# A list scheduler that holds a PSUM bank as one piece, and each block's attention put right ahead of its own FFN, in a one-core decoder step

## The chip, the core and the metric

One core of a Trainium2 chip runs the whole program. Its engines work side by side, each through its own queue in order: TensorE (PE, matmuls; its weight loads are shown as PEld), VectorE (DVE), ScalarE (ACT), GpSimd (POOL) and SyncE (SP), which issues every DMA. The metric is the device time of one execution in microseconds (us), lower is better.

## What is computed

One step of a hybrid decoder layer for a prompt of 2048 tokens and 8 decode tokens, all in float32, D = 1024. Cut to what matters:

```python
def decoder_layer(x, ...):
    y, ... = parallel_mixer(rms_norm(x, norm_mix), ...)      # conv module (31 taps) beside gated DeltaNet, 4 heads
    x = x + y                                                # y = concat(conv, delta) @ w_out
    x = x + memory_attend(rms_norm(x, norm_mem_q), mem_k, mem_v, w_mq, w_mo)   # 4 heads, 256 memory tokens
    x = x + swiglu(rms_norm(x, norm_ffn), w_gate, w_up, w_down)                # D_FF = 2816
    return x, ...
# and rms_norm(x, norm_f) at the end; the decode tokens attend to 8 cached memories of 256 tokens
```

## The kernel before, in words

The prompt is cut into 4 blocks of 512 tokens (`NB`, `TB`). First the mixer runs over two pairs of blocks (PE tiles `hd`, `glua`, `glub` for the projections; `pk`, `pq`, `pu`, `pch`, `po` for the DeltaNet chunks). Then each block has three more steps: the output projection ("out", PE tile `rg` reading `catS`), the memory attention ("att": scores `sc`, softmax, transposes `ppt`, and the product with the values, PE tile `rg` reading `pT`), and the FFN (`fx`, `fy`, `fz` for gate and up, `dn` for down). The FFN is a Strassen-like scheme: its right operands `op` are halves and differences (`xn`, `tt`) that DVE and ACT build from the normalised block. Every large weight is split into two float32r parts, a high one by ACT and a low one by POOL or DVE (tile `w` from `raw`). The decode attention (`kt`, `scs`, `psc`, `podd`) runs as one more lane beside the FFN of block 0.

The Python code writes no instruction at once. `Tape` records all of them with their operands (`add`, L165) in program order, and `Tape.order` (L283) then lays them out by list scheduling: it walks a clock of its own for each engine with the costs of `cost` (L176) and the latencies `LAT`, takes for each engine the ready operation with the smallest key, and the order in which operations are taken is the order in which each engine's queue receives them. What is ready follows from `graph` (L227): reads and writes of a tile depend on each other where their boxes (`box`, L207) overlap. In a PSUM tile, which is one bank, two column ranges are so two independent pieces, and nothing in the planner stops one engine from reading a bank while another writes another part of it. The program itself does not run that way: in the trace no two engines are ever in one PSUM tile at the same time.

Program order around the change: `att_plan` and `out_plan` (L855 to L872) put the weights in the order out(0), att(0), out(1), att(1), FFN(0), out(2), att(2), FFN(1), out(3), att(3), FFN(2), held `dn` of FFN(2), FFN(3); the loop at the end of `hybrid_step` (L2754 to L2780) runs the same order. `ffn_norm` (L2536) builds the operands `op` of a block's FFN as a lane of its own; its wait `may` holds it back until the FFN ahead is done and the next block's scores are taken. `dec_attend` (L2286) waits for free tiles of the `t2` pool. `chj` (L1668, L1680, L1810) is the unused output of ACT's squares, in a single buffer.

## Time and profile before

| | us |
|---|---|
| median of 3 runs (3053.68 to 3060.42) | 3055.63 |
| the profiled execution | 3056.0 |
| its span, first to last instruction | 3054.3 |
| PE busy in it | 2958.2 (97%) |
| DVE / POOL / ACT busy | 1971.5 / 1380.7 / 1325.6 |

The mean granted TensorE clock is 0.988 of full speed. A table of windows gives, for each stretch of the span, the busy time of each engine in it with the number of its instructions, the granted clock (PEclk, 1.00 is 2.4 GHz, 0.50 is 1.2 GHz), the DMA engines' share and what they moved. A waits view says which engine sat idle ahead of which tile, and what it had waited for. A timeline lists instructions in order of time; in brackets stands the idle time just before and its releaser. All instructions carry one line, L450, since the tape issues them all there; so they are told apart by tiles.

### The profile page before, as it was taken

What the parts mean: (1) busy time and instruction counts of PE and PEld (TensorE: products, weight loads), DVE (VectorE), ACT (ScalarE), POOL (GpSimd) and SP (SyncE); (2) the same over time, 40 slices, a digit from 0 to 9 for tenths busy, and PEclk for the clock granted to TensorE, in tenths of its full rate; (3) what the DMA queues carried; (4) which work ended last, traced back from release to release, by engine and by line L of the source; (5) the groups of instructions that cost most, each with busy time, mean ns of one, the idle gap of its engine ahead of it and who ended that gap; (6) DMA issues with size and microseconds to landing.
All of it is one profiled execution on the core that took longest, in us unless ns stands there. A gap on an engine that the chain in (4) does not pass through costs nothing.

```text
span 3054.3 us, 52803 instructions
## 1 busy us (share of the span) xinstructions
PE 2958.2 (97%) x18950; PEld 2625.0 (86%) x18950; DVE 1971.5 (65%) x3946; ACT 1325.6 (43%) x2695; POOL 1380.7 (45%) x1228
## 2 busy tenths in 40 slices
PE   8999989999999999989999999999999999999998
PEld 6898867888888878789988779988878999999997
DVE  7857888888986876687678885423576333553334
ACT  6643337543565343545455354333444332433333
POOL 3433333432446455678877204355512443444444
PEclk9999989999999999999999999999999999999999
DMA  6443334543676442277667748766534766676663
GB/s 232 153 131 101 116 114 142 160 147 96 189 255 188 134 140 80 89 245 265 233 251 262 238 136 283 253 227 232 180 117 145 241 215 218 207 244 221 220 221 109
DMA packets 358631, 567.24 MB, mean 186 GB/s; under 512 B 56832, under 2 KB 155072, under 8 KB 358352
## 3 DMA queue, kind: packets, MB, share of 16 engines
q1 hardware_dynamic: 358368, 563.86, 55.9%
q8 instruction: 150, 2.46, 0.3%
q14 instruction: 113, 0.93, 0.1%
HBM read 455.68 MB, written 108.64 MB: 185 GB/s over the span
## 4 chain that ended last, share of the span: by engine, by line
PE 72%; DVE 7%; DMA 4%; ACT 1%; issue 1%; POOL 1%; SPq 0%; POOLq 0%; DVEq 0%; ACTq 0%
PE dn L450 16%; PE fy L450 12%; PE rg L450 9%; PE fz L450 8%; PE fx L450 8%; PE sc L450 5%; PE hd L450 4%; DVE cacc L450 2%; PE pu L450 2%; PE glub L450 1%; PE glua L450 1%; DVE bit L450 1%; PE pch L450 1%; DMA Tm<-zt 1%; DMA w<-sums 1%
## 5 line engine op out<-in xcount | busy, mean ns | idle before, releaser
L450 POOL TENSOR_TENSOR w<-raw,w 128x512 fp32r<-128x512 f32 x683 | 931.4, 1369 | 955.0 <-ACT w L450 866.7
L450 ACT ACTIVATE w<-raw 128x512 fp32r<-128x512 f32 x912 | 568.3, 631 | 942.9 <-PE dn L450 231.9
L450 PE MATMUL dn<-ff,w 128*128 128x512 f32 (+2 forms) x2688 | 518.2, 346 | 0.8 <-ACT ffs L450 0.8
L450 PEld LDWEIGHTS dn<-ff,w 128*128 128x128 f32 x2688 | 421.5, 188 | 58.8 <-ACT ffs L450 1.0
L450 PE MATMUL fy<-op,w 128*128 128x256 f32 (+1 forms) x3168 | 426.8, 283 | 0.5 <-DMA w<-sums 0.5
L450 PEld LDWEIGHTS fy<-op,w 128*128 128x128 f32 x3168 | 403.0, 189 | 8.5 <-issue 1.4
L450 PE MATMUL hd<-hT,w 128*128 128x512 f32 (+2 forms) x1920 | 399.6, 359 | 8.8 <-ACT w L450 6.6
L450 DVE SCALAR_TENSOR_TENSOR cacc<-cu,cw,cacc 128x512 f32<-128x512 f32 x480 | 358.7, 747 | 16.2 <-ACT cacc L450 11.0
L450 PEld LDWEIGHTS hd<-hT,w 128*128 128x128 f32 x1920 | 306.4, 191 | 52.6 <-ACT w L450 6.8
L450 PE MATMUL fz<-op,w 128*128 128x256 f32 (+1 forms) x2112 | 286.4, 282 | 4.2 <-DMA w<-sums 2.1
L450 PE MATMUL fx<-op,w 128*128 128x256 f32 (+1 forms) x2112 | 285.7, 283 | 2.9 <-DVE op L450 1.6
L450 PEld LDWEIGHTS fx<-op,w 128*128 128x128 f32 x2112 | 270.9, 189 | 12.8 <-DVE op L450 2.1
L450 PEld LDWEIGHTS fz<-op,w 128*128 128x128 f32 x2112 | 265.9, 189 | 8.9 <-issue 3.9
L450 DVE TENSOR_TENSOR w<-raw,w 128x512 fp32r<-128x512 f32 x229 | 217.8, 959 | 69.6 <-ACT w L450 67.3
L450 DVE TENSOR_TENSOR x<-dn,x 128x512 f32<-128x512 f32 (+1 forms) x248 | 139.8, 567 | 174.9 <-PE dn L450 172.5
L450 POOL TENSOR_TENSOR sqj<-sqj,sqj 128x512 f32<-128x512 f32 (+1 forms) x98 | 130.2, 1328 | 266.9 <-ACT sqj L450 264.7
L450 PE MATMUL sc<-w,hT 128*128 128x512 f32 x768 | 193.2, 404 | 3.0 <-DVE w L450 1.8
L450 PE MATMUL rg<-catS,w 128*128 128x512 f32 (+2 forms) x960 | 191.9, 355 | 1.9 <-DVE x L450 1.9
L450 PE MATMUL rg<-pT,w 128*128 128x512 f32 x768 | 190.6, 399 | 0.3
L450 PEld LDWEIGHTS rg<-catS,w 128*128 128x128 f32 x960 | 153.9, 189 | 26.9 <-DVE x L450 2.2
L450 PEld LDWEIGHTS sc<-w,hT 128*128 128x128 f32 x768 | 142.7, 191 | 37.6 <-ACT pr L450 3.1
L450 PEld LDWEIGHTS rg<-pT,w 128*128 128x128 f32 x768 | 141.4, 188 | 33.6 <-ACT pr L450 3.0
(381 smaller groups left out, 4036.3 us busy)
## 6 DMA issues: line engine op xcount, KB each, us to landing
w<-sums SPq DMA_DIRECT2D x264, 512.0 KB, 4.4
raw<-in_w_gate_dram SPq DMA_DIRECT2D x176, 256.0 KB, 3.4
sums<-w SPq DMA_DIRECT2D x88, 512.0 KB, 3.2
raw<-in_w_down_dram SPq DMA_DIRECT2D x176, 256.0 KB, 3.4
raw<-in_w_up_dram SPq DMA_DIRECT2D x110, 256.0 KB, 2.7
raw<-in_w_in_dram SPq DMA_DIRECT2D x96, 256.0 KB, 2.8
raw<-in_w_out_dram SPq DMA_DIRECT2D x64, 256.0 KB, 3.2
raw<-wk SPq DMA_DIRECT2D x64, 256.0 KB, 2.6
```

The source lines that it names most:

```text
L450: fn(*args, **kw)
```

## The change

Four things in the scheduler, and three in the program:

- `box` returns one and the same box for every access to a PSUM tile: any two accesses of a bank depend on each other in program order if one of them writes.
- `order` also keeps, for each bank, the engine that used it last and when; an operation of another engine is put off until then plus the latency between the two (`bank_at`).
- After a pause of PE of over 1800 ns (and past 5000 ns) PE's operations cost 1.9 times as much for 3400 ns.
- An ACT operation with `accum_out` costs 92 ns more.
- Program order becomes out(0), att(0), out(1), FFN(0), att(1), out(2), FFN(1), att(2), out(3), FFN(2), att(3), held `dn`, FFN(3): a block's attention is followed by the next block's output projection and then by its own FFN. `ffn_norm` loses its wait `may`; the query norm waits for the FFN one block back, not two. The lanes that prepare the next block's `catS` and load its x (`cat_prep`, `load_x`) are started in `att_phase`, not at the end of the FFN.
- `chj` gets 4 buffers.
- The decode attention leaves `RES` = 5 more `t2` tiles free.

```diff
@@ cost
-            return 0.834 * n + (50 if psum_in else 94) + 93 * ptr, False, SETS.get(kw.get("func"))
+            return 0.834 * n + (50 if psum_in else 94) + 93 * ptr + (92 if "accum_out" in kw else 0), False, SETS.get(kw.get("func"))
@@ box
+        if a.name in self.psum:
+            return 0, 0, 0, 0
@@ order
+        banks = [[x for x in ts if x in self.psum] for ts in tiles]
+        bank = {}
+
+        def bank_at(n, e):
+            return max([bank[x][1] + self.LAT[bank[x][0]][e] for x in banks[n] if x in bank and bank[x][0] != e], default=0.0)
...
                 k, n = heappop(av)
+                at_ = bank_at(n, e)
+                if at_ > t:
+                    ready[n] = at_
+                    push(n)
+                    n = None
+                    continue
...
+            if e == "pe" and s > clock[e] + 1800 and s > 5000:
+                slow = s + 3400
+            if e == "pe" and s < slow:
+                ns *= 1.9
...
+            for x in banks[n]:
+                bank[x] = e, max(fin, bank[x][1]) if x in bank and bank[x][0] == e else fin
@@ plan of the weights
-    for b in range(2):
-        out_plan(b)
-        att_plan(b)
+    out_plan(0)
+    att_plan(0)
+    out_plan(1)
     for b in range(NB):
         ffn_plan(b)
+        if b + 1 < NB:
+            att_plan(b + 1)
         if b + 2 < NB:
             out_plan(b + 2)
-            att_plan(b + 2)
@@ three places
-            j = small("chj", [P, DK], dt=mybir.dt.bfloat16, bufs=1)
+            j = small("chj", [P, DK], dt=mybir.dt.bfloat16, bufs=4)
@@ dec_attend, five places
-                yield ("t2", 3)
+                yield ("t2", 3 + RES)
@@ att_phase, ffn (its lines that did the same for b + 2 go)
-        scored[b].append(1)
+        if b + 1 < NB and b:
+            S.add(cat_prep(b + 1, cats[b + 1]))
+            S.add(load_x(b + 1))
@@ ffn_norm
-        yield may
@@ the loop
-    attention(0)
-    attention(1)
+    output(0)
+    S.add(cat_prep(1, cats[1]))
+    S.add(load_x(1))
     for b in range(NB):
+        S.add(ffn_norm(b, att_done[b], ops[b]))
+        att_phase(b, hqs[b], att_done[b])
+        if b + 1 < NB:
+            output(b + 1)
+        else:
+            rest()
         ws.pool_lo, ws.ahead = "near", 8
         rest = ffn(b, ops[b], go[b])
         ws.pool_lo, ws.ahead = False, 4
-        if b + 2 < NB:
-            attention(b + 2)
-        elif b + 1 < NB:
-            rest()
```

How it moves the queues, at three places. PE at the transposes of q into one bank (`pq_414`, first pair of blocks, about 98 us), with what each row waits for, before and then after:

```order
L450 MATMUL hd_412<-hT_291,w_322 128x256
L450 MATMUL hd_413<-hT_291,w_322 128x264
L450 MATMUL pq_414<-ident,qTd_387 128x128 [waits DMAHW2_49]
L450 MATMUL pq_414<-ident,qTd_387 128x128 x2
L450 MATMUL pq_414<-ident,qTd_387 128x128 [waits Activation_49]
L450 MATMUL hd_412<-hT_293,w_322 128x256
```

```order
L471 MATMUL hd_412<-hT_291,w_322 128x256
L471 MATMUL hd_413<-hT_291,w_322 128x264
L471 MATMUL pq_414<-ident,qTd_387 128x128 [waits DMAHW1_49]
L471 MATMUL pq_414<-ident,qTd_387 128x128 x3
L471 MATMUL hd_412<-hT_293,w_322 128x256
```

Before, the fourth transpose comes behind ACT's square of the first columns of the same bank; now the four stand together and wait for no ACT.

PE at the transposes of the decode scores (`psc`), in the scores of the attention beside which the decode lane ends; before that is att(2), and now the transposes stand in out(2), behind att(1):

```order
L450 MATMUL sc_3739<-w_3760,hT_3744 128x512 x3
L450 MATMUL sc_3740<-w_3760,hT_3744 128x512 x3
L450 MATMUL sc_3754<-w_3760,hT_3744 128x512 x3
L450 MATMUL psc_3799<-ident,scs_3546 32x128 [waits DVE_49,PE_49]
L450 MATMUL sc_3805<-w_3765,hT_3692 128x512 [waits Activation_49]
L450 MATMUL sc_3805<-w_3765,hT_3692 128x512 x2
L450 MATMUL sc_3805<-w_3770,hT_3694 128x512 [waits Activation_49]
L450 MATMUL psc_3799<-ident,scs_3546 32x128 [waits DVE_49]
```

```order
L471 MATMUL rg_3696<-catS_3593,w_3675 128x512 x3
L471 MATMUL rg_3697<-catS_3593,w_3675 128x512 [waits PE_49]
L471 MATMUL rg_3697<-catS_3593,w_3675 128x512 x2
L471 MATMUL psc_3698<-ident,scs_3391 32x128 [waits PE_49]
L471 MATMUL psc_3698<-ident,scs_3391 32x128
L471 MATMUL rg_3694<-catS_3595,w_3677 128x512 [waits Activation_49]
```

Before, each `psc` waits for DVE; now none does, because a wait of PE ahead of it has already covered the last `scs`.

PE at the start of FFN(1), where the first product `fx` takes the operands `op`:

```order
L450 MATMUL podd_3903<-vth_3939,pb_3816 64x512 [waits Activation_49]
L450 MATMUL rg_3972<-pT_3885,w_3919 128x512 x2
L450 MATMUL fx_3984<-op_3854,w_3960 128x256 x6
L450 MATMUL fx_3984<-op_3869,w_3960 128x256
L450 MATMUL podd_3903<-vtl_3940,pb_3816 64x512 [waits DVE_49]
L450 MATMUL podd_3903<-vth_3942,pb_3815 64x512 [waits Activation_49]
L450 MATMUL fx_3984<-op_3869,w_3960 128x256 x5
```

```order
L471 MATMUL rg_3777<-catS_3607,w_3754 128x512 x3
L471 MATMUL fx_3785<-op_3737,w_3771 128x256 [waits Activation_49]
L471 MATMUL fx_3785<-op_3737,w_3771 128x256
L471 MATMUL fx_3785<-op_3737,w_3771 128x256 [waits DVE_49]
L471 MATMUL fx_3785<-op_3737,w_3771 128x256 [waits Activation_49]
L471 MATMUL fx_3785<-op_3737,w_3771 128x256 [waits DVE_49]
L471 MATMUL fx_3785<-op_3737,w_3771 128x256
L471 MATMUL fx_3785<-op_3757,w_3771 128x256 [waits Activation_49]
L471 MATMUL fx_3785<-op_3757,w_3771 128x256 [waits DVE_49]
```

Before, no `fx` waits, since the operands were built during the attention ahead; now nearly each one waits for the ACT and DVE halves of its own operand.

## Rows read from the trace of the kernel before

**Rows 1.** The page: busy time, share of the span and instructions of each engine.

```profile
PE 2958.2 (97%) x18950; PEld 2625.0 (86%) x18950; DVE 1971.5 (65%) x3946; ACT 1325.6 (43%) x2695; POOL 1380.7 (45%) x1228
```

**Rows 2.** Windows over stages: each engine's busy us, then PEclk, DMA share, GB/s.

```profile
0.00:50.00 50.00, 36.82 (x182) 27.20 (x183) 33.74 (x74) 26.05 (x46) 24.73 (x58) 0.90 0.78 264
...
404.00:453.00 49.00, 37.94 (x171) 28.73 (x170) 37.88 (x95) 14.33 (x29) 12.93 (x18) 0.77 0.40 118
453.00:850.00 397.00, 388.15 (x2136) 320.19 (x2136) 343.96 (x782) 200.97 (x434) 155.94 (x184) 1.00 0.48 148
850.00:1145.00 295.00, 275.61 (x1747) 241.23 (x1746) 233.32 (x498) 147.66 (x341) 150.31 (x138) 0.99 0.56 177
...
1300.00:1400.00 100.00, 89.46 (x622) 82.58 (x621) 83.74 (x126) 48.37 (x98) 73.70 (x52) 0.95 0.70 243
...
1745.00:1765.00 20.00, 14.08 (x51) 10.33 (x50) 16.34 (x42) 8.92 (x24) 0.00 (x0) 0.74 0.43 133
1765.00:3038.00 1273.00, 1269.11 (x8799) 1170.43 (x8798) 579.56 (x1166) 474.03 (x905) 505.49 (x382) 1.00 0.61 206
3038.00:3054.30 16.30, 3.88 (x21) 2.77 (x20) 9.21 (x22) 2.30 (x6) 5.58 (x8) 0.72 0.39 130
```

**Rows 3.** The waits of PE over the span: us in total, times, longest.

```profile
PE pq L450 <- ACT chj L450: 5.2, 6, 1.8
...
PE lnq L450 <- ACT lny L450: 1.9, 2, 1.4
...
PE pkk L450 <- DVE zd L450: 1.2, 1, 1.2
...
PE pk L450 <- ACT chj L450: 1.0, 2, 0.5
PE pkk L450 <- DVE lt L450: 1.0, 2, 0.5
```

**Rows 4.** Timeline from 97 us: start us, us, engine, instruction.

```profile
97.93 0.49 PE L450 MATMUL pq<-ident,qTd 128*128 128x128 f32 x3
...
100.20 0.33 PE L450 MATMUL pq<-ident,qTd 128*128 128x128 f32 x1 [1.77 <-ACT chj L450]
```

**Rows 5.** Timeline of PE from 404 us, between the mixer's two pairs.

```profile
414.96 1.87 PE L450 MATMUL pss<-ones,sqj 128*128 128x1 f32 x8 [2.75 <-POOL sqj L450]
...
427.74 0.85 PE L450 MATMUL hd<-hT,w 128*128 128x512 f32 x3
```

**Rows 6.** The waits of PE from 1300 to 1400 us, around FFN(0)'s start.

```profile
PE lnp L450 <- DMA lnx<-cvT: 3.5, 1, 3.5
PE fx L450 <- DVE op L450: 1.6, 2, 1.2
...
PE fx L450 <- ACT ffu L450: 0.7, 2, 0.4
```

**Rows 7.** Timeline of PE from 1746 us, in the scores of att(2).

```profile
1753.74 0.39 PE L450 MATMUL psc<-ident,scs 128*32 128x128 f32 x1 [4.09 <-DVE scs L450]
...
1757.25 3.36 PE L450 MATMUL sc<-w,hT 128*128 128x512 f32 x7 [1.84 <-DVE w L450]
```

**Rows 8.** Tiles of FFN(1)'s operands: ns min/median/max, first and last start.

```profile
L450 DVE SCALAR_TENSOR_TENSOR xn<-x,vcol,rsb x8: 740/744/747, 1787.7 to 1811.1; 128x512 f32<-128x512 f32 x8
...
L450 DVE TENSOR_TENSOR op<-xn,op x8: 415/548/684, 1793.7 to 1813.1; 128x256 fp32r<-128x256 f32 x4, 128x512 fp32r<-128x512 f32 x4
...
L450 DVE TENSOR_TENSOR tt<-xn,tt x8: 414/416/420, 1794.6 to 1813.7; 128x256 f32<-128x256 f32 x8
...
L450 DVE TENSOR_TENSOR op<-tt,op x8: 682/682/686, 1795.9 to 1815.2; 128x512 fp32r<-128x512 f32 x8
```

**Rows 9.** The chain of waits from 1679 us: start us, us, what.

```profile
1679.22 5.55 PE rg L450 x24
```

**Rows 10.** DVE's low weight parts: the tile's instructions, then its group 1100 to 1400.

```profile
L450 DVE TENSOR_TENSOR w<-raw,w x229: 657/693/1815, 6.6 to 2689.1; 128x512 fp32r<-128x512 f32 x115
...
L450 DVE TENSOR_TENSOR w<-raw,w 128x512 fp32r<-128x512 f32 x24 | 27.5, 1159 | 3.6 <-ACT w L450 3.6
```

More of the change, by code (lines that the diff above doesn't have):

```diff
@@ L332, in order @@
         clock = dict.fromkeys(engines, 0.0)
-        dma_at, port_at, table = 0.0, 0.0, None
+        dma_at, port_at, table, slow = 0.0, 0.0, None, 0.0
+        banks = [[x for x in ts if x in self.psum] for ts in tiles]
+        bank = {}
+        def bank_at(n, e):
+            return max([bank[x][1] + self.LAT[bank[x][0]][e] for x in banks[n] if x in bank and bank[x][0] != e], default=0.0)
         start, end, ends = [0.0] * N, [0.0] * N, {}
@@ L379, in order @@
                     if e == "dve" and self.ops[n][7][1] and port_at > t + 150 and not skipped:
-                        other = [(k2, m) for k2, m in av if not self.ops[m][7][1] and all(x in given for x in tiles[m])]
+                        other = [(k2, m) for k2, m in av if not self.ops[m][7][1] and all(x in given for x in tiles[m]) and bank_at(m, e) <= t]
                         if other:
@@ L1679, in dn_front @@
         for c in range(NT):
-            j = small("chj", [P, DK], dt=mybir.dt.bfloat16, bufs=1)
+            j = small("chj", [P, DK], dt=mybir.dt.bfloat16, bufs=4)
             A.activation(out=j, in_=pq[:, c, :], func=AF.Square, accum_out=ssq[:, 4 + c : 5 + c])
@@ L1809, in dn_chain @@
             Sst[h] = Sn
-            j = small("chj", [P, DK], dt=mybir.dt.bfloat16, bufs=1)
+            j = small("chj", [P, DK], dt=mybir.dt.bfloat16, bufs=4)
             A.activation(out=j, in_=po[:, c, :], func=AF.Square, accum_out=m4[:, c : c + 1])
@@ L2308, in dec_attend @@
         yield scs
-        yield ("t2", 1)
+        yield ("t2", 1 + RES)
         yield ("ps", "s")
@@ L2322, in dec_attend @@
         yield pe
-        yield ("t2", 2)
+        yield ("t2", 2 + RES)
         pbs = [t2("pb", dt=F32R) for _ in range(2)]
@@ L2346, in dec_attend @@
                 for mc in range(2):
-                    yield ("t2", 3)
+                    yield ("t2", 3 + RES)
                     vt, vh, vl = t2("vtd"), t2("vth", dt=F32R), t2("vtl", dt=F32R)
@@ L2358, in dec_attend @@
                     drop(vt, vh, vl)
-            yield ("t2", 1)
+            yield ("t2", 1 + RES)
             pr = t2("pvr", (64, TB))
@@ L2534, in halves, with ffn_norm @@
         return v if n is None else v[:, :, :n]
-    def ffn_norm(b, done, op, may):
+    def ffn_norm(b, done, op):
         xs, w, res = xt_[b], width(b), {}
@@ L2652, in product @@
                     go_on.append(1)
-                    if b + 2 < NB:
-                        S.add(cat_prep(b + 2, cats[b + 2]))
-                        S.add(load_x(b + 2))
         fin = set()
@@ L2753, in hybrid_step @@
     att_done = {b: set() for b in range(NB)}
-    go, scored = ({b: [] for b in range(-2, NB)} for _ in range(2))
-    go[-2].append(1)
+    go = {b: [] for b in range(-1, NB)}
     go[-1].append(1)
@@ L2759, in output @@
         done = set()
-        S.add(norm_q(lambda: xt_.get(b), done, hqs[b], lambda: go[b - 2]))
+        S.add(norm_q(lambda: xt_.get(b), done, hqs[b], lambda: go[b - 1]))
         out_phase(b, cats[b], done)
-    def attention(b):
-        output(b)
-        if b == 0:
-            S.add(cat_prep(1, cats[1]))
-            S.add(load_x(1))
-        S.add(ffn_norm(b, att_done[b], ops[b], lambda: go[b - 1] and (b + 1 == NB or scored[b + 1])))
+    output(0)
+    S.add(cat_prep(1, cats[1]))
+    S.add(load_x(1))
+    rest = None
+    for b in range(NB):
+        S.add(ffn_norm(b, att_done[b], ops[b]))
         att_phase(b, hqs[b], att_done[b])
-    attention(0)
-    attention(1)
-    for b in range(NB):
+        if b + 1 < NB:
+            output(b + 1)
+        else:
+            rest()
         ws.pool_lo, ws.ahead = "near", 8
@@ L2776, in hybrid_step @@
         ws.pool_lo, ws.ahead = False, 4
-        if b + 2 < NB:
-            attention(b + 2)
-        elif b + 1 < NB:
-            rest()
     S.until(lambda: not S.lanes, "end")
```

## The prediction, made before the changed kernel ran

> **What bounds the kernel now.** I read the page first. PE is busy 2958.2 of 3054.3 us [rows 1], so it sits idle 96.1 us, and no order of the same 18950 matmuls can give back more than that, apart from what the clock costs. The windows by stage [rows 2] show where it goes: the window less PE's busy time is the idle part, and one less PEclk, times the window, is about what the lower clock takes (1.00 is 2.4 GHz). The head (0 to 50) has 13.2 us idle and the tail (from 3038) 12.4 us; the tail's queue is unchanged and the head's nearly so, so both stay. From 404 to 453, between the mixer's two pairs, 11.1 us are idle, and the clock of 0.77 takes about 11.3. From 850 to 1145 (memory keys and values, out(0), att(0)) 19.4 us are idle. From 1300 to 1400, where FFN(0) starts, it is 10.5 and about 5.0 of clock; from 1745 to 1765, inside att(2), 5.9 and about 5.2. From 1765 to 3038 only 3.9 us are idle in 1273. So FFN and attention at their present places have nearly nothing to give, and what can be won lies ahead of 1765. There DVE is the second limit: 344 of 397 us busy from 453 to 850, with PE idle for 8.9 [rows 2].
>
> **The change part by part.** *Banks.* The waits view of PE shows five groups in which PE waits for ACT or DVE in the middle of filling a bank [rows 3]: pq 5.2, lnq 1.9, pkk 1.2 and 1.0, pk 1.0, in sum 10.3 us. One of them in the timeline: three transposes into pq end at 98.4, and the fourth starts at 100.20, after 1.77 us idle, once ACT has read the first columns [rows 4]. The planner of before let that happen since it saw columns, not a bank. In the new queue the four transposes stand together with no wait on ACT (the first pair of fences), and the same holds for all banks of pk, pq, pkk and lnq. So these waits go; what is late next is the DeltaNet chain that follows on DVE, which is 87% busy there. I take 8 of the 10.3 as won; the bounds are 0 (the chain is as late as before) and 10.3.
>
> *404 to 453.* Both queues leave the second pair's projections waiting for its norm. Before, pss (the sum of squares) starts at 414.96 after waiting 2.75 us for POOL, and the projections at 427.74 [rows 5], with DeltaNet steps scattered among them afterwards. Now all four steps of that head's chain stand ahead of pss's result, and one more square (sqj) has to be added on POOL first. That starts the projections later by one or two such steps, some 2 us, and takes away the chain's waits among the projections, some 4. I take -2; bounds -6 to +6, half of the idle time there either way.
>
> *Start of FFN(0).* Before, its operands come just ahead of their use: fx waits 1.6 us for op and 0.7 for ffu [rows 6], and each such pause lowers the clock a little. In the new order att(0) is done earlier, out(1) lies in between, and the operands of the first product are built 15 us or more of PE work ahead of their use. So 2.3 us of waits go and with them about a third of the 5.0 us of clock: -4. The DMA wait of lnp (3.5 us) has nothing to do with it and stays. But the last DeltaNet chunks and the convolution of the second pair, which had att(1) beside them, now lie beside FFN(0); the bounds are -9 and +8 (about half of the stage's 15.5, lost or lost again).
>
> *The decode scores.* In att(2) PE stands 4.09 us at psc until DVE has made the last scs, and soon after 1.84 at sc for a weight part from DVE [rows 7]. Now psc stands in out(2), with no wait on DVE of its own (the second pair of fences). The 4.09 us go, and about 3 of the clock's 5.2: -7. The 1.84 has its like in the scores of att(1), where DVE has the softmax and the same 32 products kt, and stays. Bounds -9 and 0.
>
> *Starts of FFN(1) and FFN(3).* This is what the new program order costs. Before, the last op of FFN(1) starts at 1815.2 [rows 8], well ahead of its use behind att(2), and its fx waits for nothing (third pair of fences). Now between the norm of block 1 and fx there is only what is left of out(2): 90 rg rows at 5.55 us for 24 [rows 9] are 20.8 us, with two small products 21.5. In it DVE has to do 8 xn at 0.744, 16 tt at 0.416 (of which the row shows 8), 8 op at 0.548 and 8 at 0.682 [rows 8], which makes 6.0 + 6.7 + 4.4 + 5.5 = 22.6 us, and about six residual adds of some 0.7 us besides: 26.8. That is 5.3 too much; the last op pieces (some 2.5) are not needed by the first product, so 2.8, with some clock 3.5. FFN(3) is covered by some 29 us of held dn, but has 14 residual adds, and more weight parts of att(3) are on DVE; 3.5 again. FFN(2) has operands 13 us or more ahead. So +7; bounds 0 and +20 (each start two thirds of the worst in the trace, the 15.5 us of 1300 to 1400).
>
> *The rest.* 45 weight operations move from POOL to DVE, 45 x 0.69 [rows 10] or 31 us, most of them in att(3), where DVE has the room; 0, and +3 if they hold up that start. The buffers of chj, the cost of accum_out and RES only move ACT and lane times: 0. The half-rate rule costs nothing on the chip; it only changes the planner's choice, and PE's queue up to out(1) is nearly the same as before, except from 404 to 470 and around 900 to 1050.
>
> The sum: -8 - 2 - 4 - 7 + 7 = -14. The profiled execution took 3056.0 us (1.7 outside the span), 0.4 above the median, so the sum stands against it as it is: **3042 us**. With its bounds and not all of them at once, 3029 to 3049.
>
> **The rivals.** *Starts that starve (slower).* The operands' DVE work is late by more than I count, as at the start of FFN(0) before. If FFN(1) and FFN(3) each cost that stage's 15.5 us, that is +31, and with the bank waits half won (-5) and the decode scores (-5) the time is 3056 + 31 - 10 = 3077. Slower than before begins where the two starts together cost over 21 us, all other terms as forecast. For it speaks that fx there waits on nearly every operand; against it that out(2) and the held dn cover most of the DVE work.
>
> *DVE and POOL in each other's way (no change).* The same DVE weight part takes 0.69 us in the median and 1.16 from 1100 to 1400 [rows 10], where POOL is busy with weights. The new order puts convolution, DeltaNet and FFN(0) into one stretch of about 100 us in which DVE's work, at the durations of the rows, already adds up to about 100. If some 30 more operations there take 0.47 us longer, DVE is 14 us late and PE with it: 3056. The Trainium skill (SBUF — State Buffer, Who interferes with whom) says that a DVE instruction with two SBUF inputs and a GpSimd one that reads SBUF block each other for a whole instruction; the trace agrees for the weight part. It speaks against this part of the change, since it brings more pairs of that kind together.
>
> *More than the sum (faster).* With banks and ACT's accumulations counted rightly, the DVE and ACT queues of the whole mixer are laid out anew, while PE's stays. If that gives back half of the idle time from 404 to 453 and from 850 to 1145, about 15 us, and two dips of the clock, about 5, the time is 3022. Against it: chains of DeltaNet there need DVE's time, whatever its order.
>
> *The rules do nothing.* The banks' waits are filled by others and the order of blocks is even: 3053. It goes with the no change.
>
> **How the numbers follow.** The forecast has 0.45. Starving starts have 0.18, DVE and POOL or rules without effect 0.22, more than the sum 0.15. A measurement of this kernel tells 0.2%, about 6 us, from no change, so faster is under 3049.5 and slower over 3061.7: faster 0.45 + 0.15 = 0.60, same 0.22, slower 0.18. The range leaves out the far half of the two outer cases: 3014 to 3070.
>
> **What would show it.** In the profile after: no wait of PE on chj at pq and pk, none on lny at lnq; psc without the 4 us; from 404 to 453 about as much idle as before; fx waiting for op at the starts of FFN(1) and FFN(3), 2 to 5 us each, and hardly any at that of FFN(0). PE's busy time stays near 2950 and its idle falls to about 82. Wrong would be the forecast if these two starts show over 10 us each with a lower clock, if the stretch of FFN(0) has DVE full and PE idle for over 20 us, or if the waits of the mixer only change their names.

## The result, and the profile after

The changed kernel takes 3025.07 us (median of 4 executions, 3019.55 to 3026.84), the kernel before beside it 3056.39 us. The ratio is 0.9893, with a 95% interval of 0.9876 to 0.9911: about 31 us or 1.1% faster. (The ratio is formed over the executions and not from the two medians, so the two can differ a little.) The forecast was 3042, 14 us faster, in a range of 3014 to 3070: the sign and the range held, the size did not, as the gain is more than twice the one forecast.

The profiled execution took 3023.58 us, its span 3021.9, so 32.4 us less span than before. The page's first part, to set beside [rows 1]:

```profile
PE 2950.2 (98%) x18950; PEld 2625.5 (87%) x18950; DVE 1965.6 (65%) x3991; ACT 1317.9 (44%) x2696; POOL 1336.3 (44%) x1183
```

PE's busy time is near 2950 us, as the forecast had it, but its idle time fell from 96.1 to 71.7 us and not to 82. That is 24.4 us; the other 8.0 us are in PE's busy time. The mean granted clock, 0.989 after 0.988, makes up some 3 of them (an estimate, 0.001 of 3022 us); the rest is not explained. Windows of after, with the columns of [rows 2]; up to 1145 us they are stretches of nearly the same work:

```profile
50.00:404.00 354.00, 348.89 (x2390) 316.16 (x2389) 274.41 (x657) 174.70 (x383) 136.68 (x164) 1.00 0.43 130
404.00:453.00 49.00, 44.29 (x189) 33.24 (x188) 41.76 (x77) 20.16 (x40) 18.87 (x26) 0.85 0.45 143
...
850.00:1145.00 295.00, 281.59 (x1766) 246.92 (x1764) 211.38 (x467) 141.51 (x333) 150.86 (x137) 0.99 0.52 160
1145.00:1300.00 155.00, 150.75 (x1069) 139.03 (x1068) 147.16 (x242) 80.34 (x164) 117.07 (x89) 1.00 0.70 240
...
1861.00:1904.00 43.00, 39.62 (x232) 31.96 (x231) 23.60 (x37) 21.42 (x41) 25.86 (x20) 0.92 0.73 236
...
2640.00:2670.00 30.00, 27.32 (x203) 26.65 (x203) 25.95 (x75) 12.01 (x22) 13.65 (x10) 0.83 0.42 133
```

From 404 to 453 PE is idle for 4.7 us (11.1 before) and the clock is 0.85 (0.77 before); from 850 to 1145 it is idle for 13.4 (19.4 before). The stretch from 1145 to 1300 now holds the start of FFN(0): 4.2 us idle and a clock of 1.00, against 10.5 and 0.95 where that start stood before [rows 2]. New are two weak places: 1861 to 1904, in FFN(1), and 2640 to 2670, at the start of FFN(3).

**One table for all kernels.** The stages stand at other times in each kernel, so the experiments are compared by the loss of PE: the time from the start of one product to the start of the next, less what that product takes when PE runs without a pause (0.2327 us for 128x512, 0.119 for 128x256, as in the FFN, where the loss over 400 us of work is under 1 us). It holds idle time and the lower clock alike. The stages are cut at equal amounts of PE work, in us of such undisturbed products; all kernels have 2907 of them. Up to 1100 the work is the same in all of them ("pair 1" to 350, "mixer" 350 to 1100); from 1100 to 1900 stand att(1), out(2), att(2), FFN(0) and FFN(1) in the order of each kernel, from 1900 to 2700 the rest up to FFN(3)'s start, behind that the tail with 12.4 to 14.2 everywhere. The losses of a row are those of one execution; the executions of one kernel spread over 2 to 19 us, mostly some 10, so a stage is told apart by several kernels and not by one. The traced execution can also lie off its kernel's median: that of handover_2ns is 10 us above it, those of chj_only and after_bank 8 and 7 us below. Each group of kernels was timed beside executions of the kernel before of its own, whose medians went from 3052.23 to 3056.77; so across the table the ratios compare, and the medians only roughly.

| kernel | bank rule | blocks | median us | ratio (95%) | pair 1 | mixer | 1100 to 1900 | 1900 to 2700 |
|---|---|---|---|---|---|---|---|---|
| before | no | old | 3056.39 | 1 | 22.8 | 65.7 | 34.3 | 5.1 |
| after | yes | new | 3025.07 | 0.9893 (0.9876 to 0.9911) | 14.8 | 51.7 | 20.2 | 9.4 |
| bank_only | yes | old | 3024.23 | 0.9909 (0.9890 to 0.9929) | 12.0 | 51.2 | 30.8 | 3.6 |
| rules_only | yes | old | 3042.92 | 0.9969 (0.9955 to 0.9984) | 15.0 | 54.1 | 42.1 | 2.4 |
| order_only | no | new | 3042.20 | 0.9974 (0.9955 to 0.9993) | 19.9 | 64.0 | 21.6 | 10.4 |
| chj_only | no | old | 3042.51 | 0.9962 (0.9949 to 0.9975) | 21.3 | 53.5 | 30.0 | 1.9 |
| before_2ns | no | old | 3048.61 | 0.9990 (0.9977 to 1.0003) | 20.9 | 61.4 | 36.6 | 3.2 |
| bank_2ns | yes | old | 3034.38 | 0.9941 (0.9918 to 0.9964) | 18.4 | 56.3 | 35.9 | 3.5 |
| after_bank | yes | new | 3024.14 | 0.9902 (0.9881 to 0.9924) | 12.4 | 47.7 | 19.8 | 9.1 |
| after_no_half | yes | new | 3022.84 | 0.9898 (0.9875 to 0.9921) | 15.6 | 54.7 | 21.6 | 7.7 |
| box_only | box alone | old | 3057.18 | 1.0013 (0.9999 to 1.0027) | 17.5 | 77.5 | 30.3 | 2.7 |
| handover_only | handing over alone | old | 3024.66 | 0.9908 (0.9891 to 0.9924) | 14.4 | 50.5 | 28.5 | 3.5 |
| after_bank_pool | yes | new | 3031.66 | 0.9927 (0.9910 to 0.9945) | 13.9 | 49.7 | 22.6 | 12.0 |
| after_no_res | yes | new | 3019.97 | 0.9890 (0.9873 to 0.9908) | 13.9 | 52.3 | 16.4 | 10.8 |
| after_2ns | yes | new | 3042.25 | 0.9957 (0.9943 to 0.9971) | 16.1 | 61.4 | 24.0 | 7.1 |
| handover_2ns | handing over alone | old | 3038.11 | 0.9936 (0.9915 to 0.9957) | 20.7 | 59.3 | 37.7 | 3.5 |
| box_2ns | box alone | old | 3044.95 | 0.9965 (0.9954 to 0.9976) | 19.0 | 59.4 | 35.9 | 2.3 |
| after_fused | yes | new | 3021.50 | 0.9887 (0.9869 to 0.9905) | 19.3 | 50.4 | 24.7 | 5.4 |
| after_minus_2ns | yes | new | 3028.31 | 0.9910 (0.9893 to 0.9926) | 18.5 | 56.5 | 23.5 | 9.0 |
| combined | yes | new | 3015.39 | 0.9871 (0.9853 to 0.9888) | 15.5 | 47.0 | 19.6 | 8.5 |

So the 32 us between the two traces are: pair 1 -8.0, mixer -14.0, 1100 to 1900 -14.1, 1900 to 2700 +4.3, tail -0.2.

### The profile page after: what moved, and what is told of

Read it like the earlier page. It is cut to its first block, busy times and chain, and to the rows that moved or that the text cites. A ratio compares the mean times of both kernels' runs of the same rounds, so it can differ in the third digit from the quotient of the medians.

```text
span 3021.9 us, 52713 instructions
## 1 busy us (share of the span) xinstructions
PE 2950.2 (98%) x18950; PEld 2625.5 (87%) x18950; DVE 1965.6 (65%) x3991; ACT 1317.9 (44%) x2696; POOL 1336.3 (44%) x1183
## 4 chain that ended last, share of the span: by engine, by line
PE 79%; DVE 11%; DMA 6%; ACT 2%; issue 1%; POOL 0%; SPq 0%; POOLq 0%; DVEq 0%; ACTq 0%
PE dn L471 15%; PE fy L471 12%; PE rg L471 10%; PE fz L471 8%; PE fx L471 8%; PE hd L471 7%; PE sc L471 4%; DVE cacc L471 3%; PE glub L471 2%; PE glua L471 2%; PE pu L471 2%; DVE bit L471 1%; PE pch L471 1%; DVE x L471 1%; DMA vp<-jn 1%
## 5 line engine op out<-in xcount | busy, mean ns | idle before, releaser
L471 POOL TENSOR_TENSOR w<-raw,w 128x512 fp32r<-128x512 f32 x639 | 868.6, 1365 | 949.5 <-ACT w L471 899.4
L471 PE MATMUL hd<-hT,w 128*128 128x512 f32 (+2 forms) x1920 | 397.8, 358 | 10.5 <-ACT w L471 5.7
L471 DVE TENSOR_TENSOR w<-raw,w 128x512 fp32r<-128x512 f32 x273 | 233.0, 860 | 103.7 <-ACT w L471 97.6
L471 PEld LDWEIGHTS rg<-catS,w 128*128 128x128 f32 x960 | 154.5, 189 | 24.7 <-issue 1.4
```

Source lines behind the costliest of these rows:

```text
L471: fn(*args, **kw)
```

## The experiments

**The parts of the change.** Theory A was that the bank rule lays the mixer's queues out anew and that the mixer's gain is all its own; B was the prediction's own step, that just the waits inside a bank go; C that the block order is the gain; D that the half-rate rule and the cost of accum_out count. E concerned the buffers of `chj`.

*bank_only.* The kernel before with the lines of the diff under `box`, and those under `order` that name `banks`, `bank` and `bank_at`; nothing else of the change.

```diff
+        if a.name in self.psum:
+            return 0, 0, 0, 0
...
+                at_ = bank_at(n, e)
+                if at_ > t:
+                    ready[n] = at_
+                    push(n)
...
+            for x in banks[n]:
+                bank[x] = e, max(fin, bank[x][1]) if x in bank and bank[x][0] == e else fin
```

> The kernel before with the bank rule alone (one box per PSUM tile, and an engine put off until another has left the bank); cost of accum_out, half rate, chj, RES and block order as before. Theory A (the rule lays the mixer's queues out anew and nearly all of the mixer's gain is its own): 3033 to 3040 us, idle time of PE ahead of 1145 us lower by about 15 us. Theory B (the prediction's step: only the waits inside a bank go, 8 us): 3045 to 3050. Theory C (the rule does little, the gain comes from block order): 3053 to 3057.

3024.23 us, ratio 0.9909: within the interval as fast as the whole change, and faster than any of the theories had it. Of the 30 us between its loss and that of before, 25 are in pair 1 (-10.8) and the mixer (-14.5, nearly all of it from 350 to 450 us of work); FFN(0)'s start and the decode scores stay nearly as they were. For this list C falls, and B is too small.

*rules_only.* The whole change in the scheduler and in `chj`, on the old program and with the old RES.

```diff
+            return 0.834 * n + (50 if psum_in else 94) + 93 * ptr + (92 if "accum_out" in kw else 0), ...
+            if e == "pe" and s > clock[e] + 1800 and s > 5000:
+                slow = s + 3400
-            j = small("chj", [P, DK], dt=mybir.dt.bfloat16, bufs=1)
+            j = small("chj", [P, DK], dt=mybir.dt.bfloat16, bufs=4)
```

> The kernel before with all four planner rules and the four chj buffers, but the old block order and the old RES. Theory A: 3033 to 3040, like the bank rule alone, the rest of the change's 31 us being block order. Theory B: 3043 to 3048. Theory D (the half-rate rule and accum_out matter as well): at least 5 us below the bank rule alone.

3042.92 us: 19 us slower than with the bank rule alone. A is missed by 3 us; B's time came, at its lower edge, but with the mixer's gain (65.7 to 54.1), which B doesn't have. The mixer is 3 us worse than in bank_only, and from 1100 to 1900 it is 11 us, most of it at one place: PE stands there for 6.4 us at the decode values `podd`, which wait for the two parts, high and low, of the cached memory. On the new order the same additions cost nothing that can be told (after_bank and the changed kernel, below). This was the first sign that a list is partly a draw; whether the added rules or the draw made it slower isn't shown.

*order_only.* The changed kernel with the scheduler and `chj` of before: block order, `ffn_norm` and RES alone.

```diff
-        if a.name in self.psum:
-            return 0, 0, 0, 0
...
-                at_ = bank_at(n, e)
```

> The changed kernel with the planner's four rules and chj as before: block order, ffn_norm without its wait, RES = 5 alone. Theory A: 3042 to 3047 (minus 10: the starts of FFN(0) and the decode scores minus 12 and minus 11, the late starts of FFN(2) and FFN(3) plus 9 and plus 8, the latter two as in the changed kernel). The prediction's terms for order alone (minus 4, minus 7, plus 7): 3052. Theory C: 3025 to 3030.

3042.20 us, ratio 0.9974, 8 us faster. By stages: 1100 to 1900 -12.7, 1900 to 2700 +5.3, and the mixer nearly as before (-1.7), as theory A had it.

*chj_only.*

```diff
-            j = small("chj", [P, DK], dt=mybir.dt.bfloat16, bufs=1)
+            j = small("chj", [P, DK], dt=mybir.dt.bfloat16, bufs=4)
```

> The kernel before with four buffers for chj and nothing else; PE's queue differs from the old one only here and there. PE's waits for ACT's chj are 14.4 us in sum before and none after. Theory E (the single buffer made those waits): they go, 3042 to 3047. Theories A and B (the waits are for ACT's reading of the bank, whatever the buffer): within 3 us of 3056, with the waits for chj still over 10 us.

The waits of PE on `chj` stay, as A and B said. Two rows of the waits view of PE (us in total, times, longest):

```profile
PE pq L450 <- ACT chj L450: 6.5, 8, 2.0
...
PE pk L450 <- ACT chj L450: 3.7, 8, 0.5
```

They are even longer than in [rows 3]: it is ACT's reading of the bank that PE waits for, not the unused output. But the time fell to 3042.51: theory E's time without its cause. The gain sits in the mixer (65.7 to 53.5, in an execution 8 us faster than the median), where the queue differs from the old one only here and there. So a list without the bank rule can win in the mixer about what the changed kernel wins there.

**How much is the draw.** A list scheduler takes one of many near-equal orders. Theory L says that any touch of its numbers moves the mixer by several us. The touch is one line in `cost`:

```diff
-            return 68 + (61 if ptr else 0) + n * (6.2 if op == "reciprocal" else 0.525 if half else 1.042), big > 1, None
+            return 70 + (61 if ptr else 0) + n * (6.2 if op == "reciprocal" else 0.525 if half else 1.042), big > 1, None
```

*before_2ns* and *bank_2ns* have this line on the kernel before and on bank_only.

> A control: the kernel before, with DVE's fixed cost in the planner at 70 ns in place of 68, and nothing else. No rule is better or worse by it; it only shakes the list. Theory L (the mixer's time is partly the luck of the list: any touch of the planner moves it): 3056 plus or minus 5 to 15 us, the stages from 350 to 1145 us each moving by 3 us or more. Theory A (the gain is the bank rule's doing): within 3 us of before.

> The kernel bank_only with the same 70 in place of 68. Theory A: within 3 us of bank_only, 3021 to 3027. Theory L: the part of the first pair of blocks (8 to 10 us, seen in all three kernels with the rule and in none without) stays, the rest is thrown anew: 3022 to 3045, with most of the difference between 350 and 1145 us.

The kernel before hardly moves in sum (0.9990), but its stages do: from 350 to 450 us of work it loses 9 us less, in the rest of the mixer 5 more, as theory L had it. bank_only loses 10 us (3034.38), and A's 3021 to 3027 is missed. The windows from 404 to 453 of before_2ns and of chj_only, to set beside [rows 2] and the row of after:

```profile
404.00:453.00 49.00, 41.72 (x195) 30.94 (x195) 45.40 (x104) 18.67 (x39) 18.72 (x23) 0.86 0.43 128
```

```profile
404.00:453.00 49.00, 44.13 (x218) 34.11 (x218) 45.38 (x93) 21.49 (x43) 17.86 (x23) 0.90 0.49 153
```

Without the bank rule PE is idle there for 7.3 and 4.9 us at a clock of 0.86 and 0.90; the kernel before has 11.1 and 0.77, the changed one 4.7 and 0.85.

With 70 the bank rule is worth 0.49% (0.9941 against 0.9990, 15 us), with 68 it was worth 0.91%. Not even the first pair's part is safe: it is 18.4 here, against 20.9 without the rule.

*after_bank* is the changed kernel less half rate, accum_out and the four buffers; *after_no_half* less the half-rate rule only:

```diff
-            if e == "pe" and s > clock[e] + 1800 and s > 5000:
-                slow = s + 3400
-            if e == "pe" and s < slow:
-                ns *= 1.9
```

> The changed kernel without the half-rate rule, the cost of accum_out and the four chj buffers: the bank rule and the new program order alone. Theory A: parts add, bank_only less what order_only wins over before: 3024 - 10 = 3014 (3009 to 3019). Theory L: mixer thrown anew, 3012 to 3032. Theory D (half rate and accum_out carry a part of the gain): over 3030.

> The changed kernel without the half-rate rule alone. Theory D: 5 us or more slower than the changed kernel, over 3030, and most of it where PE pauses (the head, 404 to 453). Theory L: 3025 plus or minus up to 10, with as many stages better as worse. The prediction's step (the rule costs and wins nothing): within 3 us of 3025.

Both are level with the changed kernel (3024.14, 3022.84): D falls, and the half-rate rule does nothing that can be told. The parts don't add either: bank_only and order_only together would have given 3014. In after_bank the stages from 1100 on do look as in order_only, but the timed median doesn't show it; theory A's 3009 to 3019 is missed.

**Which half of the rule.** *box_only* has just the first hunk of bank_only, *handover_only* everything of bank_only but that hunk.

```diff
+        if a.name in self.psum:
+            return 0, 0, 0, 0
```

> The kernel before with half of the bank rule: one box per PSUM tile, no putting off of an engine. PE never comes back to a bank that another engine has begun to read, as in bank_only. If the first pair's gain is that order alone: idle and clock loss of the first pair of blocks 12 to 18 us (before 23), total 3030 to 3047. If the handing over has to be counted too: first pair 20 to 23 us, 3045 to 3056.

> The kernel before with the other half: boxes by columns as before, but an engine put off until the bank is left plus the latency. 13 of the 14 returns of PE to a bank go all the same. If either half is enough: first pair 12 to 18 us, 3030 to 3047. If the order of the box is what counts: first pair 20 to 23, 3045 to 3056. If putting off works against the list (engines are held for what the chip doesn't ask): slower than before, over 3062.

box_only takes 3057.18, and handover_only 3024.66, 5 us below any of its forecasts. A window of the kernel before over the first pair of blocks (columns as in [rows 2]):

```profile
50.00:404.00 354.00, 345.09 (x2347) 311.54 (x2346) 265.03 (x614) 169.54 (x373) 127.71 (x156) 1.00 0.41 128
```

The windows of box_only over the first pair and from 404 to 850:

```profile
50.00:404.00 354.00, 348.94 (x2374) 315.79 (x2374) 265.31 (x624) 172.34 (x378) 128.12 (x159) 1.00 0.43 130
404.00:850.00 446.00, 427.57 (x2310) 350.20 (x2310) 382.06 (x871) 215.05 (x466) 171.70 (x203) 0.97 0.47 143
```

The same windows of handover_only:

```profile
50.00:404.00 354.00, 349.37 (x2401) 317.24 (x2400) 274.96 (x657) 174.22 (x381) 134.15 (x166) 1.00 0.43 133
404.00:850.00 446.00, 436.60 (x2388) 360.27 (x2389) 392.50 (x871) 226.04 (x486) 177.16 (x205) 0.99 0.50 154
```

The box does what was forecast of the rule: the waits of PE on `chj` at pq and pk fall from 6.2 to 0.3 us, and its idle time in the first pair from 8.9 to 5.1 us. (Of its forecast the first pair, 17.5, fits the first case and the time the second, since the mixer loses 11.8 us more than before.) DVE gets no further for it: it has done 624 instructions of 265.31 us, before 614 of 265.03. With the handing over counted, PE is idle for 4.6 us, and DVE has 657 instructions of 274.96 us behind it: 10 us of work ahead. In the next 446 us PE then stands for 9.4 us in place of 18.4. This lead of DVE is a mark of the handing over: by 404 us DVE has done 614 to 638 instructions in the six kernels without the handing over, and 648 to 661 in thirteen of the fourteen with it (627 in after_minus_2ns).

**Is it the draw again?** *handover_2ns*, *box_2ns* and *after_2ns* have the 70 in handover_only, box_only and the changed kernel; *after_minus_2ns* has 66 in the changed kernel.

> handover_only with 70 in place of 68. If putting engines off carries the gain: 3020 to 3037, first pair of blocks 12 to 18 us, mixer behind it 48 to 57. If handover_only was a lucky draw: 3040 to 3057.

> box_only with 70 in place of 68. If the box alone gives nothing beyond the first pair's waits: 3043 to 3057, mixer behind the first pair 58 to 78 us. If box_only was an unlucky draw and either half is enough: 3025 to 3040.

> The changed kernel with DVE's fixed cost in the planner at 70 ns in place of 68: a second draw of the changed kernel's list. If 31 us were what the change is worth: 3022 to 3028. If this draw was lucky, as the other kernels' stages suggest (about 20 us by their means): 3030 to 3040.

> The changed kernel with DVE's fixed cost in the planner at 66 ns in place of 68: a third draw. If 3025 is what the change gives and 70 was the odd draw: 3020 to 3029. If 68 was the lucky one: 3034 to 3045. In between, near 3032, the change is worth some 20 us with a scatter of 8.

3038.11, 3044.95, 3042.25 and 3028.31. So with 70 the two halves are 7 us apart and not 33, and the changed kernel gives back 17 of its 31 us. By ratios the halves are 9 us apart. after_minus_2ns came as if 3025 were what the change gives, after_2ns above both of its ranges, and handover_2ns between its two, with more loss in the mixer (59.3) than if putting off carried the gain. Of the same windows of after_2ns, the first and the last:

```profile
50.00:404.00 354.00, 345.86 (x2363) 312.49 (x2361) 273.99 (x650) 168.79 (x380) 136.03 (x165) 1.00 0.43 131
...
850.00:1145.00 295.00, 274.63 (x1711) 239.43 (x1709) 223.61 (x489) 137.97 (x328) 142.17 (x130) 0.98 0.51 160
```

The lead is there (650 instructions), but it doesn't carry to the end of the mixer: PE is idle for 20.4 us in the last window, against 13.4 in the changed kernel. By ratios the three draws of the change are worth 1.07%, 0.90% and 0.43%, on average 0.80% or 24 us, and the two draws of before differ by 0.10%. Over all kernels, pair 1 and mixer lose 60 to 80 us with the handing over counted (14 kernels, mean 69) and 75 to 95 without (6 kernels, mean 84). So the handing over goes with 15 us less on average, but the two groups overlap, and what it does inside the mixer is not shown: with 70 the halves lose the same in these stages (box_2ns 78.4, handover_2ns 80.0) though only the second has DVE's lead (648 instructions and 625; but its traced execution is 10 us above its median), and after_minus_2ns, without the lead, loses 75.0.

The block order is told more surely. From 1100 to 1900 the ten kernels with the new order lose 16.4 to 24.7 us (mean 21) and the ten with the old one 28.5 to 42.1 (mean 34); from 1900 to 2700 it is 5.4 to 12.0 (mean 9) after 1.9 to 5.1 (mean 3). No row of one group reaches into the other: the order wins some 13 us and gives back some 6.

**The late places.** *after_bank_pool* is after_bank with one line more, which puts 39 low weight parts of att(3) and the held `dn` on POOL:

```diff
+        if b == NB - 1:
+            ws.pool_lo = True
         att_phase(b, hqs[b], att_done[b])
```

> after_bank (bank rule and new order alone) with the low weight parts of att(3) and of the held dn on POOL, 39 of them, none on DVE ahead of FFN(3). If the late start of FFN(3) comes from DVE having weight parts beside the operands: its 6.6 us fall to 1 to 3 and the time is 3024 - 5 = 3019. If the operands alone are too much for DVE: 5 to 7 us stay, 3022 to 3026. If POOL's weights slow DVE by the port: the same or worse, 3024 to 3030.

3031.66 us, by the medians 7 us slower than after_bank (the intervals of the ratios overlap) and a little over the port's 3024 to 3030, and the stage of FFN(3)'s start (2540 to 2700 us of work) loses 9.3 us where it lost 6.6. Groups of DVE from 2630 to 2660 us in the changed kernel (busy us, mean ns of one):

```profile
L471 DVE TENSOR_TENSOR x<-dn,x 128x256 f32<-128x256 f32 x26 | 10.5, 414 | 0.0
L471 DVE SCALAR_TENSOR_TENSOR xn<-x,vcol,rsb 128x512 f32<-128x512 f32 x6 | 5.4, 912 | 0.0
...
L471 DVE TENSOR_TENSOR xd<-dn,xd 128x4 f32<-128x4 f32 x26 | 3.9, 151 | 0.0
...
L471 DVE TENSOR_TENSOR w<-raw,w 128x512 fp32r<-128x512 f32 x4 | 2.7, 682 | 0.0
L471 DVE TENSOR_TENSOR tt<-xn,xn 128x256 f32<-128x256 f32 x3 | 1.2, 415 | 0.0
```

The same groups in after_bank_pool:

```profile
L467 DVE TENSOR_TENSOR x<-dn,x 128x256 f32<-128x256 f32 x28 | 11.3, 411 | 0.1
...
L467 DVE SCALAR_TENSOR_TENSOR xn<-x,vcol,rsb 128x512 f32<-128x512 f32 x4 | 4.9, 1216 | 0.0
...
L467 DVE TENSOR_TENSOR tt<-xn,xn 128x256 f32<-128x256 f32 x2 | 2.2, 1113 | 0.0
```

With weights on POOL the same `tt` from two SBUF tiles takes 1113 ns in place of 415 and `xn` 1216 in place of 912, while the residual add, which has one input in PSUM, stays at 411; in after_bank itself it is 415 and 946. One `tt` beside one weight part of POOL, in the timeline of after_bank_pool:

```profile
2642.24 1.36 POOL L467 TENSOR_TENSOR w<-raw,w 128x512 fp32r<-128x512 f32 x1 [1.81 <-ACT w L467]
...
2642.38 1.51 DVE L467 TENSOR_TENSOR tt<-xn,xn 128x256 f32<-128x256 f32 x1
```

The Trainium skill (SBUF — State Buffer, Who interferes with whom) says just that: a DVE instruction with two SBUF inputs contends with a GpSimd one that reads SBUF, one with at most one SBUF input, outside its 2-port modes, does not. The trace agrees. In the 30 us of the changed kernel four weight parts take 2.7 us of DVE and 26 pairs of residual adds 14.4, so the adds are the larger load; the next run tries them.

*after_fused* sums the two held groups of each output tile in one bank, so that 16 pairs of adds stand there and not 32; the held weights then come tile by tile:

```diff
-            for g in range(NG - HOLD, NG):
-                for m in range(KC):
-                    down(g, m)
+            for m in range(KC):
+                pts = [pm("dn", (P, hi - lo)) for lo, hi in spans]
+                for g in gs:
+                    ...
+                        three(pts, wk(held[g], 0, at), wk(held[g], 1, at), hact[f], spans, g == gs[0] and n_ == 0, ...)
+                ws.free(1 + m % 2)
+                add_half(m, pts)
```

> The changed kernel with the two held groups of FFN(2)'s down projection summed in one bank for each output tile, so that DVE adds 16 pairs (x and decode columns, 0.41 + 0.15 us) ahead of FFN(3) in place of 32; PE's products are the same. If the residual adds make FFN(3) late: DVE has 9 us less there, the stage's 8.9 us fall to 0 to 3, total 3025 - 7 = 3018. If the operands' own chain is late: 6 to 9 stay and the time is 3022 to 3028.

The adds in the same 30 us:

```profile
L471 DVE TENSOR_TENSOR x<-dn,x 128x256 f32<-128x256 f32 x12 | 4.9, 417 | 0.8 <-PE dn L471 0.7
...
L471 DVE TENSOR_TENSOR xd<-dn,xd 128x4 f32<-128x4 f32 x12 | 1.8, 151 | 0.0
```

The stage of FFN(3)'s start (2540 to 2700) loses 4.6 us in place of 8.9, and the kernel takes 3021.50, ratio 0.9887, which is within the interval of the changed one. The adds that went are half of that stage's loss; 4.6 us remain, of which an `ffu` of DVE holds PE for 1.3, so the result lies between the two forecasts.

*after_no_res* takes RES out of the decode attention:

```diff
-                yield ("t2", 3 + RES)
+                yield ("t2", 3)
```

> The changed kernel with the decode attention leaving no t2 tiles free, as before the change; its scores then come 10 us of PE work earlier, its values up to 30. If RES makes the decode values late beside FFN(1) (6.8 us near 1893): that loss falls to 1 to 3, 3020. If it is the place beside FFN(1) itself: 5 to 8 us stay, 3023 to 3029. If RES saved the attention from waiting for tiles, as in rules_only, where podd waited 14 us: over 3032.

3019.97 us, 5 us less by the medians, but level by the ratios (0.9890 after 0.9893). In the stage from 1600 to 1900, which holds the decode values, the loss falls from 9.3 to 3.7. So in this list RES held the lane back into a worse place; that the kernel gets faster by it isn't shown. That no RES is better in general doesn't follow: rules_only, also without it, lost 23.2 in this stage on the old order.

*combined* is after_bank with no RES in the decode attention and with the fused held groups:

> after_bank (bank rule and new order) with no RES in the decode attention and the held groups summed in one bank: where the parts add, 3024 less 4 (after_no_res against the changed kernel) less 4 (after_fused against it), 3016; by the draw of the list 3008 to 3030.

3015.39 us, ratio 0.9871 (0.9853 to 0.9888), faster than the kernel before by 1.3%. By the medians it is 10 us less than the changed kernel, by the ratios 7, and the two intervals overlap (0.9876 to 0.9911 there), so that it is faster than the changed kernel isn't shown. As one draw it may owe some of its time to its list.

## Why the prediction was right or wrong

Term by term, forecast and then measured between the two traces: banks -8 and -8.0; 404 to 453 -2 and -7.4; the rest of the mixer 0 and -6.6; FFN(0)'s start -4 and -11.8; the decode scores with FFN(1)'s start -3.5 and -2.3; FFN(3)'s start +3.5 and +4.3. What failed is the mixer behind the first pair (12 us) and FFN(0)'s start (8 us).

**Banks, -8 (bounds 0 to -10.3): right for this trace.** The four transposes of [rows 4] now run without a wait. PE's timeline of after:

```profile
97.55 0.60 PE L471 MATMUL pq<-ident,qTd 128*128 128x128 f32 x4
```

No wait of PE on `chj` is left at pq or pk, and pair 1 lost 8.0 us less. The Trainium skill (PSUM — Partial Sum Buffer, PSUM bank collisions raise a hardware error) says that the chip itself doesn't make an engine wait at a bank, and that the dependency has to be in the program; here it is, as the wait for ACT that stands at the fourth pq of before. (In the trace of before this can be seen at pk, pq, pkk and lnq, where no ACT or DVE instruction on the tile overlaps one of PE; other names stand for several banks at once, so it isn't shown for them.) Over all kernels pair 1 loses 15.8 us on average with the handing over and 20.2 without it, 4.5 less: before has the most loss there of all twenty (22.8), so the full 8 is partly this list. The sum of the waits that the view names, 10.3 us, was taken as all that the rule could give. With the handing over counted the planner also gives DVE other work in the time in which it would have stood in line for a bank (657 instructions by 404 us after 614); what that lead is worth behind pair 1 is not shown.

**404 to 453, -2 (bounds -6 to +6): the step that failed first.** The stage at this place lost 7.4 us less (25.2 to 17.8 from 350 to 450 us of work), and in bank_only 14.5 less. The forecast reasoned from the place of PE's rows (four steps ahead of pss) at the durations of before, and took as its sign that the stretch is idle about as long as before; it is idle for 4.7 us and not 11.1. That the bank rule did this is not shown. Without the rule, before_2ns loses 9 us less there and chj_only 11, with 619 and 638 instructions of DVE by 404 us, while order_only and box_only lose nearly what before does. So the place was bad in the list of before, and lists with and without the rule leave it; the cause stays open.

**The mixer from 453 to 1145, taken as 0: the second.** It was left out of the sum since PE's queue is nearly the same there, and came to -6.6. The bank rule alone doesn't give that: from 450 to 1100 us of work bank_only and handover_only lose within 1 us of before, and after_2ns loses some 5 us more than before. The rival "more than the sum" named these stages and a new layout of the DVE and ACT queues, at 20 us and with a chance of 0.15. The mixer gave 12 us beyond the sum. That the rival's time, 3022, nearly came is partly luck, since the rest is from FFN(0)'s start. Here a term was missing in the sum: a rule that holds in all stages was priced only where its wait has a name. On average over all kernels the mixer loses 53 us with the handing over and 64 without it, so 10 us where the sum has 2.

**FFN(0)'s start, -4 (bounds -9 to +8): too small.** From 1100 to 1600 the loss fell by 11.8 us. Most of it is the order's own: the ten kernels with the new order lose 11 to 16 us there and the ten with the old one 17 to 25, and order_only loses 8 us less than before in this stage. Three pieces were mis-sized. The clock gives back all of its 5.0 us and not a third: it is 1.00 there, with 4.2 us idle and no wait of fx over 1.5. The DMA wait of `lnp` (3.5 us, [rows 6]) "has nothing to do with it and stays", said the text; it is not among the waits of after, nor of order_only, nor of bank_only on the old order. Of the 2.3 us of waits the 1.6 for `op` went, and the 0.7 for `ffu` became 1.5. What waits there now, in PE's waits from 1145 to 1300:

```profile
PE fx L471 <- ACT ffu L471: 1.5, 1, 1.5
PE fx L471 <- DVE w L471: 0.9, 1, 0.9
```

**The decode scores, -7: right, and half given back.** psc [rows 7] now follows without a wait:

```profile
1646.99 0.38 PE L471 MATMUL psc<-ident,scs 128*32 128x128 f32 x2
```

But the next piece of that lane, the values `podd`, now ends inside FFN(1) at a place where PE waits for their split and for a prepared weight:

```profile
1886.70 0.44 PE L471 MATMUL podd<-vth,pb 128*64 128x512 f32 x1 [0.82 <-ACT vth L471]
...
1895.81 0.39 PE L471 MATMUL fz<-op,w 128*128 128x256 f32 x1 [1.80 <-DMA w<-sums]
```

With the clock of 0.92 from 1861 to 1904 that stretch loses some 7 us. The forecast moved psc and never asked where the rest of its lane went. Net of both, 1600 to 1900 gave 2.3.

**The starts of FFN(1) and FFN(3), +3.5 each: the sum right, the halves not.** FFN(1) starts without a loss (0.1 us around 1600 us of work), but not because DVE's work fitted beside out(2): the first fx starts at 1691.49 us, while the last `op` of ACT starts at 1697.0 and the last of DVE at 1697.7, so some 6 us of the work did come behind it, about as counted. PE waits for none of it: all of it, and not just 2.5 us, are pieces that the first products don't take. FFN(3) costs 7.6 more than before. PE's row there:

```profile
2659.06 2.50 PE L471 MATMUL fx<-op,w 128*128 128x256 f32 x10 [2.68 <-DVE w L471]
```

"14 residual adds" was the slip: the block carries the decode columns, so each held `dn` is added in two halves of two pieces, 32 pairs at 0.41 and 0.15 us, 18 us of DVE and not some 10. after_fused, with half of them, halves the stage's loss.

**The rest, 0: not refuted** for the half-rate rule and accum_out (after_no_half and after_bank are level with the changed kernel); as to the waits, right for `chj`, though chj_only took 0.38% off by its list. Of the rivals, the starving starts came at FFN(3) alone and cost half of what was asked there; DVE and POOL in each other's way is not seen to hold PE up in the change; in after_bank_pool it slowed the operands.

**And the draw.** The forecast of 14 us was of a change in general, the measured 31 of one list. A step of 2 ns in a planner's cost gives lists of the same change at 3025, 3028 and 3042. So part of the miss, some 7 us against the mean of the three draws, is this list and not the change in general; the rest of it, about 10 us, is the mixer and FFN(0)'s start above, and some of that may be the list of before, as chj_only shows. By the means of the table, which are rough since the lists have much in common, the handing over is worth some 15 us and the new order some 7, in sum 22. What stays open is why this draw is better than the 70 one: DVE's lead at 404 us is nearly the same in both (657 and 650), nearly all of the 12.5 us between the two traces stands from 450 to 1100 us of work, no wait there was found that is the cause by itself, and three draws give the mean only roughly.

## What to carry to other kernels

Price a change in a planner's model not only at the waits that it removes by name: every stage whose queues it lays out anew gets a term and a wide bound. A stage that is bad in one list may be good in the next without any better rule, so look at it in a second list of the kernel before. Before a gain of under 1% from a list scheduler is believed, shake the list (one cost by 2 ns) and compare draws with draws; and try several lists for the final kernel, since the best draw is a gain of its own. When a lane is moved, follow all its later pieces, and count the pieces of an add that its layout splits.

## What the runs showed that was not expected

A pause cost more than itself here: the wait of 2.68 us at FFN(3)'s start stands in a stage that loses 8.9 us, with a clock of 0.83 from 2640 to 2670 (about 5 us of the loss by that, an estimate) and one more wait of 1.5 us behind it. Between kernels of equal PE work and equal rules, 2 ns in a planner's number of 68 moved the median by up to 17 us, more than the executions of one kernel mostly spread.
